# A float32 decoder block on one core: wider runs for the FFN's up tiles, Strassen sums in three batches, and an opening in pieces

## The chip, the cores and the metric

The kernel runs on one core of a Trainium2 chip. Its time is the device time of one execution in microseconds (us), as a median of runs; less is better. The core has a matrix engine (TensorE, PE in the profile, with its weight loads as PEld), a vector engine (VectorE, DVE), an activation engine (ScalarE, ACT), GpSimd (POOL) and SyncE (SP). SP does no arithmetic here: it issues nearly all loads, in order, and each may wait until a buffer is free. Each engine works through its own instructions in order, and they wait for one another by semaphores.

## The reference

One decoder block on 256 tokens of width 2048, all in float32. `c` gives six vectors (shift, scale and gate of both halves) by a product with a 2048 x 12288 matrix; the rest is three large products with pointwise work between them.

```python
mod = jax.nn.silu(c) @ w_ada[l] + b_ada[l]
sh1, sc1, g1, sh2, sc2, g2 = jnp.split(mod, 6, axis=-1)
h = modulate(rms_norm(x, norm1_g[l]), sh1, sc1)
proj = h @ w_in[l]                                  # 2048 x 6144: q, k, v, gb, gc, xt
...                                                 # attention over the one block of 256; short gated convolution
x = x + g1[:, None, :] * (mixed @ w_out[l])         # 2048 x 2048
h2 = modulate(rms_norm(x, norm2_g[l]), sh2, sc2)
u = causal_dwconv(h2 @ w_ffn_up[l], ffn_conv_w[l], ffn_conv_b[l])   # 2048 x 11264, 3 taps
u_gate, u_up = jnp.split(u, 2, axis=-1)
ffn = (jax.nn.silu(u_gate) * u_up) @ w_ffn_down[l]  # 5632 x 2048
x = x + g2[:, None, :] * ffn
```

## The kernel before

**Slots.** All large products run weight tile by weight tile. A tile holds 4 blocks of 128 x 512 (1 MB) in a `raw` buffer; there are seven. ACT rounds it to `hi` (`split_hi`, L329), DVE subtracts to get `lo` (`split_lo`, shown as L166, the line through which most DVE work is issued), and PE multiplies hi by hi, hi by lo and lo by hi. There are three `hi` and three `lo` buffers, and both are made two slots ahead. Such a tile is a slot; the program has 228. PE's order is the order of the slots, written out before anything is issued. All other work is put at a slot by `at(slot, f)`, and within a slot the table `cls` sorts it. The tables in `CFG` thus set the order on every engine.

**Loads.** `want` queues an issue, `load_next` issues one when a buffer comes free, and SP issues in that order. `x_first` and the table `ada` decide how the tiles of `w_ada` (read for the six vectors) are mixed into those of the slots. A `w_ada` tile is multiplied on PE (`ada` L396) or added up on DVE (`ada` L389).

**The opening.** Scale and shift of the first half (SC1, SH1) come first, for two of the 16 row blocks only (256 columns): two tiles of 1 MB each, 8 x 128 x 256 values per partition. PE sums them into 4 x 32 equal rows, ACT copies the sums (`adae`), PE transposes them (`adac`), DVE reduces the transposed rows to two columns (`adaz`), and ACT adds the shift to `hf` to get `h`. The products of slot 0 (`mc`, L583) follow, first with the halves of the first weight tile that are rounded by then.

**The FFN's up products.** `w_ffn_up` has 22 groups of 256 columns on the gate side and 22 on the up side. A unit is one group of both: each of its tiles is loaded by two DMAs of 512 KB (runs of 1 KB), and four such tiles (2048 rows) fill four PSUM banks `z` (L1048, L1063, L1066). PSUM has eight banks. Behind a unit's last product, `up_sum` copies the right half of each bank by ACT and adds the left by DVE (`ub`), which frees the bank. Then both sides are convolved (`up_conv`, `up_conv_b`: `uy`, `tap`), the gate side goes through silu, and `up_gate` multiplies.

**The down products by Strassen.** Groups 0 to 15 go through one level of Strassen's scheme: per group and per half of the output columns (cp 0, 1) an A slot with three products and a B slot with four, which sum over a batch of groups in three or four PSUM banks `u`. At the end of a batch the banks are copied (`pu`, L940) and added to `down_sums` in DRAM by POOL's DMAs. `join_load` reads the sums back on SP, `join_sum` combines them. These slots stand between up slots. The last twelve tiles are ordinary products for groups 16 to 21, and the evacuation of the last bank ends the program.

## Time and profile before

| | |
|---|---|
| median of 3 runs | 1145.72 us (1144.72 to 1145.93) |
| profiled execution | 1145.98 us, of which the span 1144.2 us |
| mean granted PE clock | 0.997 |
| PE, PEld | 1129.7 us (99%), 954.1 us (83%) |
| DVE | 1064.4 us (93%), 1167 instructions |
| ACT | 731.6 us (64%), 1091 instructions |
| POOL | 61.5 us (5%) |
| DMA | 198687 packets, 363.66 MB, mean 318 GB/s |

A busy time is the time in which the engine has an instruction running, and its share is of the span. Matmuls overlap in PE, so "mean ns of one" is longer than the distance from one to the next. A row of a group gives line, engine, operation, output and inputs by name, count, busy us, mean ns of one, and the idle time just before, with what ended it. A window's row gives for each engine its busy time, then PE's granted clock, the busy share of the 16 DMA engines and GB/s.

### The profile page before, as it was taken

To read this page: it belongs to the slowest core of one execution; us is meant where nothing else is said; L and a number is where in the kernel's file an instruction comes from. 1 tells how busy PE (TensorE), PEld (TensorE's weight loads), DVE (VectorE), ACT (ScalarE), POOL (GpSimd) and SP (SyncE) were. 2 spreads that over 40 slices of the span, in tenths; PEclk is the share of its full clock that TensorE was granted. 3 is DMA by queue.
4 is the path that set the end of the run, shared out by engine and by line. 5 is a ranking of instruction groups with operands and counts; after the bars stand their busy time and mean duration, and the time that the engine had idled before them with its cause. 6 is when DMAs were issued, how large, how long until landed. Compare 5 with 4: busy or idle time off the path is not lost.

```text
span 1144.2 us, 16252 instructions
## 1 busy us (share of the span) xinstructions
PE 1129.7 (99%) x6035; PEld 954.1 (83%) x6035; DVE 1064.4 (93%) x1167; ACT 731.6 (64%) x1091; POOL 61.5 (5%) x90
## 2 busy tenths in 40 slices
PE   6999999999999999999999999999999999999998
PEld 4777778888888879988888888888888888888887
DVE  4789989989999998889999999899999999999798
ACT  4644455576786555566687676776677768866731
POOL 1000000000000000000000000101011101111000
PEclk8999999999999999999999999999999999999999
DMA  9999998998998899987679887999899988999951
GB/s 361 407 412 397 412 371 302 408 382 308 331 397 314 290 317 359 325 278 245 213 246 369 305 293 248 310 360 299 313 272 340 317 317 265 351 313 303 367 222 74
DMA packets 198687, 363.66 MB, mean 318 GB/s; under 512 B 9408, under 2 KB 108180, under 8 KB 194000
## 3 DMA queue, kind: packets, MB, share of 16 engines
q1 hardware_dynamic: 189152, 343.44, 82.8%
q0 software_dynamic: 8160, 17.04, 6.9%
q10 hardware_dynamic: 1296, 2.16, 0.6%
q8 instruction: 47, 0.77, 0.2%
q14 instruction: 32, 0.26, 0.1%
HBM read 343.70 MB, written 18.89 MB: 317 GB/s over the span
## 4 chain that ended last, share of the span: by engine, by line
PE 94%; DVE 2%; DMA 2%; issue 1%; ACT 1%; SPq 0%; DVEq 0%; ACTq 0%
PE z L1063 24%; PE z L1066 13%; PE u L1002 4%; PE u L1004 4%; PE u L1000 4%; PE z L1048 4%; PE ada L396 1%; DVE lo L166 1%; PE mx L516 1%; PE mq L516 1%; PE mg L516 1%; PE mk L516 1%; PE mx L517 1%; PE mv L516 1%; PE mg L517 1%; PE mq L517 1%
## 5 line engine op out<-in xcount | busy, mean ns | idle before, releaser
L329 ACT ACTIVATE hi<-raw 128x2048 fp32r<-128x2048 f32 (+1 forms) x227 | 417.6, 1857 | 263.6 <-DMA raw<-in_w_in_dram 73.5
L166 DVE TENSOR_TENSOR lo<-raw,hi 128x2048 fp32r<-128x2048 f32 (+2 forms) x229 | 501.6, 2200 | 23.3 <-ACT hi L329 23.1
L1063 PE MATMUL z<-h,hi 128*128 128x512 f32 x1280 | 303.3, 390 | 0.3 <-DVE ub L166 0.3
L1063 PEld LDWEIGHTS z<-h,hi 128*128 128x128 f32 x1280 | 237.8, 188 | 49.5 <-ACT hi L329 0.8
L389 DVE SCALAR_TENSOR_TENSOR ada<-raw,csil,ada 128x512 f32<-128x512 f32 (+3 forms) x167 | 195.7, 1175 | 5.3 <-DMA raw<-in_w_ada_dram 1.8
L1066 PEld LDWEIGHTS z<-h,lo 128*128 128x128 f32 x1280 | 163.1, 191 | 5.6
L1066 PE MATMUL z<-h,lo 128*128 128x256 f32 x1280 | 165.0, 283 | 0.0
L1002 PE MATMUL u<-hi,gh 128*128 128x512 f32 x224 | 88.1, 394 | 0.1
L1004 PE MATMUL u<-hi,gl 128*128 128x512 f32 x224 | 87.7, 392 | 0.0
L1000 PE MATMUL u<-lo,gh 128*128 128x512 f32 x224 | 61.4, 390 | 0.0
L812 ACT ACTIVATE uy<-ub,fc,fc 128x256 f32<-128x256 f32 x88 | 47.6, 599 | 11.9 <-DVE ub L166 11.9
L944 POOL DMA_DIRECT2D down_sums<-pu x42 | 36.7, 1290 | 304.3 <-ACT pu L940 304.3
L1002 PEld LDWEIGHTS u<-hi,gh 128*128 128x128 f32 x224 | 42.2, 188 | 10.0 <-ACT pu L940 2.9
L1000 PEld LDWEIGHTS u<-lo,gh 128*128 128x128 f32 x224 | 41.9, 188 | 9.2 <-DVE lo L166 0.3
L1004 PEld LDWEIGHTS u<-hi,gl 128*128 128x128 f32 x224 | 42.2, 189 | 7.5
L1048 PE MATMUL z<-h,hi 128*128 128x256 f32 x256 | 46.6, 284 | 0.4 <-ACT h L771 0.2
L823 ACT ACTIVATE tap<-ub,fc 128x256 f32<-128x256 f32 x96 | 41.7, 504 | 0.0
L1048 PEld LDWEIGHTS z<-h,hi 128*128 128x128 f32 x256 | 40.0, 192 | 0.8 <-ACT h L771 0.5
L166 DVE TENSOR_TENSOR ub<-z,ub 128x256 f32<-128x256 f32 x96 | 33.8, 414 | 7.2 <-ACT ub L844 7.1
L301 DVE TENSOR_TENSOR raw<-raw 128x1024 f32<-128x1024 f32 x32 | 38.9, 1217 | 1.2 <-DMA raw<-in_w_ffn_down_dram 1.2
L844 ACT ACTIVATE ub<-z 128x256 f32<-128x256 f32 x96 | 28.6, 383 | 12.7 <-PE z L1063 12.7
L1048 PE MATMUL z<-h,lo 128*128 128x256 f32 x128 | 36.2, 283 | 0.0
(460 smaller groups left out, 1787.3 us busy)
## 6 DMA issues: line engine op xcount, KB each, us to landing
raw<-in_w_ada_dram SPq DMA_DIRECT2D x96, 1024.0 KB, 7.4
raw<-in_w_ffn_up_dram SPq DMA_DIRECT2D x176, 512.0 KB, 6.1
raw<-in_w_in_dram SPq DMA_DIRECT2D x47, 1024.0 KB, 8.1
...
raw<-in_w_ffn_down_dram SPq DMA_DIRECT2D x32, 512.0 KB, 4.9
...
```

The source lines that it names most:

```text
L166: f(*a, **k)
L329: act(hi[:, :n], t[:, :n], AF.Copy)
L389: W.scalar_tensor_tensor(out=self.acc, in0=t[:, j, :], scalar=csil[:, i:i + 1], in1=self.acc, op0=ALU.mult, op1=ALU.add)
L516: mm(o, a, hi[:, k, s], start=(first and k == 0), stop=False)
L812: act(y[:, s], b[:, s], AF.Identity, bias=bias[:, i + j:i + j + 1], scale=w[2][:, i + j:i + j + 1])
L823: act(z[:, s], b[:, s], AF.Copy, scale=w[2 - d][:, i + j:i + j + 1])
L1000: mm(bank_of(key), a, lo[:, n], start=False, stop=j in ends)
L1002: mm(bank_of(key), a, hi[:, n], start=key not in begun, stop=False)
L1004: mm(bank_of(key), b, hi[:, n], start=False, stop=False)
L1048: mm(o, w[:, j, a], h2T[k + j][:, v * 256:v * 256 + 256], start=begins and j == 0 and w is hi and not v, stop=ends and j == 3 and w is lo)
L1063: mm(zp[grp][ft], hi[:, j, ft * P:(ft + 1) * P], h2T[k + j], start=begins and j == 0, stop=ends and j == 3 and not late)
L1066: mm(zp[grp][ft][:, :256], lo[:, j, ft * P:(ft + 1) * P], h2T[k + j][:, :256], start=False, stop=ends and j == 3 and late)
```

## The change

It has three parts and a new set of tables.

- **Up tiles.** A unit is now one side of two neighbouring groups: 512 neighbouring columns, one DMA of 1 MB per tile in runs of 2 KB, 88 of them in place of 176. Even units hold the gate side, odd units the up side of the same two groups. `up_sum`, `up_conv`, `up_silu` and `up_gate` are rewritten for it: a unit is followed by the convolution of both groups and, on the gate side, two silu, on the up side two products. The second tap of the gate side's convolution goes from DVE to ACT from group 6 on (`taps`).
- **Strassen batches.** Three batches of 6, 5 and 5 groups in place of four of 4: 12 half sets end in place of 16, with 42 copies `pu` in place of 56. Which Strassen slots follow which up tile (`places`) is new, and the loads and adds of the join come at other slots.
- **Opening.** The second shift tile is loaded in two pieces, and each is multiplied as it lands (`products`). Its row sums are turned into columns by two PE products with a vector `sel` in place of the two transposes and DVE's reduce, and DVE adds the first shift. The first weight tile is loaded in four pieces of 256 KB, and its four blocks are rounded by ACT and DVE in turns. `hf` is made earlier. Thirteen products of `onesr` with itself into an unused bank (`keep_busy`) stand in PE's order between the opening's products: nine behind the first scale tile, four behind the second.

All other tables (`gate_rows`, `turns`, `up`, `cls`, `x_first`, `hi_late` and so on) have new values. The number and shape of all other PE products is unchanged.

```diff
-                 [[0, 1, 2, 3], [4, 5, 6, 7], [8, 9, 10, 11], [12, 13, 14, 15]], [[0, 'A'], [1, 'A'], [0, 'B'], [1, 'B']],
+                 [[0, 1, 2, 3, 4, 5], [6, 7, 8, 9, 10], [11, 12, 13, 14, 15]], [[0, 'A'], [1, 'A'], [0, 'B'], [1, 'B']],
...
-       'join': [[-5, 1], [-2, 6]],
+       'join': [[-6, 0], [0, 4]],
-       'taps': [1, 1, 2, 6],
+       'taps': [1, 2, 2, 6],
-       'up': [[0, 2, 2, 4], [0, 0, 0, 0]],
+       'up': [[0, 1, 2, 6], [0, 2, 1, 4], [0, 1, 1, 3], [0, 0, 0, 0]],
+       'busy': [9, 4, 0],
+       'norm_at': [1, 6, 6],
...
+        def products(self, r, i, j):
+            if i == 0:
+                self.used += 1
+                self.held = self.view(take((self, r)))
+            if self.acc is None:
+                self.acc = bank(f"ada{self.part}_{self.c0}")[:, :self.n]
+            for k in range(i, j):
+                q = 32 * (k % 4)
+                mm(self.acc[q:q + 32, :], crep[:, self.rows * r + k, :], self.held[:, k, :],
+                   start=r == 0 and k < 4, stop=r == self.tiles - 1 and k >= self.rows - 4,
+                   tile_position=(0, q))
+            if j == self.rows:
+                load_next()
...
+            if not slots_begun:
+                slots_begun.append(f)
+                for j in range(4):
+                    a = (COL[f] + j % 2) * 512
+                    nc.sync.dma_start(t[:, j], w_in[0, (k + j // 2) * P:(k + j // 2 + 1) * P, a:a + 512])
+                return
...
-    def up_sum(grp, one):
+    def up_sum(u, one):
+        g, w = u // 2 * 2, u % 2
+        new = (g, w) not in ub
...
-    def conv_half(grp, w):
+    def up_conv(grp, w):
+        u = grp // 2 * 2 + w
+        y = uy[grp, w] = t2k(f"uy{grp}")
+        conv3(ub.pop((grp, w)), y, fcols[:3], fcols[3], w * 44 + 2 * grp, CFG["taps"][1 + w] if grp >= CFG["taps"][3] else 0)
...
-            slots.append((w_load(w_up, k, 4, [(grp * 256, 256), (DFF + grp * 256, 256)]), 4, go))
+            slots.append((w_load(w_up, k, 4, [(grp % 2 * DFF + grp // 2 * 512, 512)]), 4, go))
...
-            for n, f in zip(lag, (up_conv, up_conv_b, up_silu, up_gate)):
-                at(UP_SLOTS[-1] + 1 + hold + n, f, grp)
+            w = grp % 2
+            for n, (f, *a) in zip(lag, ((up_conv, 0, w), (up_conv, 1, w), (up_gate if w else up_silu, 0), (up_gate if w else up_silu, 1))):
+                at(UP_SLOTS[-1] + 1 + hold + n, f, grp - w + a[0], *a[1:])
...
+    ada_init[1].cuts[1] = [(0, 4), (4, 8)]
+    def keep_busy(b, n):
+        for _ in range(n):
+            mm(b[:, 256:384], onesr, onesr, start=True, stop=True)
...
+    sh.products(1, 0, 4)
+    keep_busy(p_one, w2)
+    sh.products(1, 4, 8)
+    rows_sum = t2k("adae")[:, :256]
+    act(rows_sum, sh.acc, AF.Copy)
+    for k in range(2):
+        mm(p_one[:, k:k + 1], rows_sum[:, k * P:(k + 1) * P], sel, start=k == 0, stop=k == 1)
+    z = small(8, "adaz")[:, :2]
+    V.tensor_copy(z, p_one[:, :2])
...
-    if CFG["first_hi"]:
-        V.tensor_copy(hi[:, s], w[:, s])
-    z, _ = ada_init[1].cols(True)
-        act(hT[k][0], h, AF.Identity, bias=z[:, k:k + 1])
+    act(hi[:, 0], w[:, 0], AF.Copy)
+            V.tensor_scalar(hT[k][0], hf[k], z[:, k:k + 1], None, op0=ALU.add)
+    V.tensor_copy(hi[:, 1], w[:, 1])
+    act(hi[:, 2], w[:, 2], AF.Copy)
+    V.tensor_copy(hi[:, 3], w[:, 3])
```

PE in the opening, from the second shift tile to the first products of slot 0, before:

```order
L396 MATMUL ada_0_219<-raw,crep 32x256 [waits DMAHW7_49]
L396 MATMUL ada_0_219<-raw,crep 32x256 x7
L453 MATMUL adac_0_268<-ident,adae_0_256 128x128 [waits Activation_49]
L453 MATMUL adac_0_268<-ident,adae_0_256 128x128
L583 MATMUL mc_293<-hi,h_261 128x512 [waits Activation_49]
L583 MATMUL mc_294<-hi,h_261 128x512 [waits PE_49]
L583 MATMUL mc_293<-hi,h_261 128x512 [waits DVE_49]
L583 MATMUL mc_294<-hi,h_261 128x512
L583 MATMUL mc_295<-hi,h_261 128x512
```

The same piece of the changed kernel (`one` is the bank of the `sel` products):

```order
L382 MATMUL ada_0_242<-raw,crep 32x256 [waits DMAHW7_49]
L382 MATMUL ada_0_242<-raw,crep 32x256 x3
L382 MATMUL ada_0_242<-raw,crep 32x256 [waits DMAHW0_49]
L382 MATMUL ada_0_242<-raw,crep 32x256 x3
L1577 MATMUL one<-sel,adae 128x1 [waits Activation_49]
L1577 MATMUL one<-sel,adae 128x1
L607 MATMUL mc_313<-hi,h_283 128x512 [waits DVE_49,Activation_49]
L607 MATMUL mc_314<-hi,h_283 128x512
L607 MATMUL mc_313<-hi,h_283 128x512 [waits DVE_49]
L607 MATMUL mc_314<-hi,h_283 128x512
L607 MATMUL mc_315<-hi,h_283 128x512 [waits DVE_49]
```

The eight shift products now wait for two loads, and `sel` products stand where the transposes stood.

SP's queue in the opening, from the tile of slot 3 to the `w_ada` tile that PE multiplies in the middle of `mq`, before (every row is 1 MB; `w_in` for slots, `w_ada` for the six vectors):

```order
L545 DMA raw<-in_w_in_dram 128x2x1024 [waits DMAHW6_49,PE_49]
L363 DMA raw<-in_w_ada_dram 128x8x256 [waits DMAHW7_49,PE_49]
L363 DMA raw<-in_w_ada_dram 128x8x256 [waits DMAHW0_49,DMAHW1_49,DVE_49,Activation_49]
L545 DMA raw<-in_w_in_dram 128x2x1024 [waits DMAHW2_49,DVE_49]
L363 DMA raw<-in_w_ada_dram 128x4x512 [waits DMAHW3_49,DVE_49]
L545 DMA raw<-in_w_in_dram 128x2x1024 [waits DMAHW5_49,PE_49]
L363 DMA raw<-in_w_ada_dram 128x4x512 [waits DMAHW4_49,DVE_49]
L363 DMA raw<-in_w_ada_dram 128x4x512 [waits DMAHW6_49,DVE_49]
L545 DMA raw<-in_w_in_dram 128x2x1024 [waits DMAHW0_49,PE_49]
L545 DMA raw<-in_w_in_dram 128x2x1024 [waits DMAHW7_49,DVE_49]
L363 DMA raw<-in_w_ada_dram 128x4x512 [waits DMAHW1_49,DVE_49]
```

The same places of the queue in the changed kernel (as many MB are ahead of the first row):

```order
L370 DMA raw<-in_w_ada_dram 128x8x256 [waits DMAHW1_49,PE_49]
L569 DMA raw<-in_w_in_dram 128x2x1024 [waits DMAHW2_49,PE_49]
L370 DMA raw<-in_w_ada_dram 128x8x256 [waits DMAHW4_49,DMAHW3_49,DVE_49]
L569 DMA raw<-in_w_in_dram 128x2x1024 [waits DMAHW5_49,DVE_49]
L370 DMA raw<-in_w_ada_dram 128x4x512 [waits DMAHW6_49,DVE_49]
L569 DMA raw<-in_w_in_dram 128x2x1024 [waits DMAHW0_49,PE_49]
L370 DMA raw<-in_w_ada_dram 128x4x512 [waits DMAHW7_49,DVE_49]
L370 DMA raw<-in_w_ada_dram 128x4x512 [waits DMAHW1_49,PE_49]
L569 DMA raw<-in_w_in_dram 128x2x1024 [waits DMAHW2_49,DVE_49]
L569 DMA raw<-in_w_in_dram 128x2x1024 [waits DMAHW3_49,DVE_49]
L370 DMA raw<-in_w_ada_dram 128x4x512 [waits DMAHW4_49,DVE_49]
```

One `w_ada` tile that PE multiplies went ahead of the tile of slot 3; the last three rows stand where they stood.

DVE at the end of an up unit with all eight banks in use (the unit's banks are `z_0_7046` to `z_3_7049`; PE's next unit begins with the bank that the first `ub` frees), before:

```order
L166 TENSOR_TENSOR gl_7147<-gs_6658,gh_7126 128x512 [waits Activation_49]
L166 TENSOR_TENSOR lo<-raw,hi 128x2048 [waits PE_49,Activation_49]
L166 TENSOR_TENSOR lo<-raw,hi 128x2048 [waits DMAHW2_49,DMAHW3_49,PE_49,Activation_49]
L389 SCALAR_TENSOR_TENSOR ada_0_4166<-raw,csil,ada_0_4166 128x2048 [waits DMAHW4_49]
L166 TENSOR_TENSOR ub_7229<-z_0_7046,ub_7229 128x256 [waits Activation_49]
L166 TENSOR_TENSOR ub_7229<-z_1_7047,ub_7229 128x256 [waits Activation_49]
L166 TENSOR_TENSOR ub_7230<-z_2_7048,ub_7230 128x256 [waits Activation_49]
L166 TENSOR_TENSOR ub_7230<-z_3_7049,ub_7230 128x256 [waits Activation_49]
```

DVE at the end of unit 7 in the changed kernel (its banks are `z_0_5407` to `z_3_5410`):

```order
L169 TENSOR_TENSOR lo<-raw,hi 128x1536 [waits DMAHW7_49,DMAHW6_49,PE_49]
L169 TENSOR_TENSOR ub_5630<-z_0_5407,ub_5630 128x256 [waits Activation_49]
L169 TENSOR_TENSOR ub_5630<-z_1_5408,ub_5630 128x256 [waits Activation_49]
L169 TENSOR_TENSOR ub_5631<-z_2_5409,ub_5631 128x256 [waits Activation_49]
L169 TENSOR_TENSOR ub_5631<-z_3_5410,ub_5631 128x256 [waits Activation_49]
L169 TENSOR_TENSOR gl_5642<-uy_4917,gh_5640 128x512 [waits Activation_49]
L169 TENSOR_TENSOR gs_5644<-uy_5087 128x256
```

And PE there in the changed kernel, from unit 7's last products to unit 8's second bank:

```order
L1090 MATMUL z_3_5410<-h_12_4539,lo 128x256 x2
L1090 MATMUL z_3_5410<-h_14_4545,lo 128x256 x2
L1087 MATMUL z_0_5665<-h_0_3718,hi 128x512 [waits Activation_49]
L1087 MATMUL z_0_5665<-h_1_3722,hi 128x512
L1087 MATMUL z_0_5665<-h_2_3729,hi 128x512
L1087 MATMUL z_0_5665<-h_3_3733,hi 128x512
L1087 MATMUL z_1_5666<-h_0_3718,hi 128x512 [waits DVE_49]
```

Unit 8 follows unit 7 with no Strassen slot between them, and its second bank waits for DVE.

More of the change, by code (lines that the diff above doesn't have):

```diff
@@ L226, in tile_block @@
     V.tensor_copy(identb, ident)
+    sel = const.tile([P, 1], F32, name="sel")
+    V.tensor_reduce(out=sel, in_=ident.rearrange("p (j r) -> p j r", j=4)[:, :, 0], axis=AX.X, op=ALU.add)
     rows(vb, [(by_p(norm1_g[0]), 16)], nc.gpsimd)
@@ L356, in __init__ @@
             self.used = 0
+            self.cuts = {}
         def want(self, r):
@@ L1504, in tile_block @@
     ada_init[0].consume(0)
+    def keep_busy(b, n):
+        for _ in range(n):
+            mm(b[:, 256:384], onesr, onesr, start=True, stop=True)
+    p_one = bank("one")
+    w0, w1, w2 = CFG["busy"]
+    keep_busy(p_one, w0)
     pr = bank("n1b")
@@ L1517, in xn_norm @@
                             in1=rT.unsqueeze(1).to_broadcast([P, 2, 256]), op=ALU.mult)
-    xn_norm(0, 1, 2, 3)
-    ada_init[0].consume(1)
-    ada_init[0].evac()
-    ada_init[0].cols()
-    xn_norm(4)
+    sc, sh = ada_init
+    n0, n1, n2 = CFG["norm_at"]
+    xn_norm(*range(n0))
+    sc.consume(1)
+    keep_busy(p_one, w1)
+    sc.evac()
+    sc.cols()
+    hf = []
+    b1 = SH1 * NK
+    for k in range(2):
+        hf.append(t1k("hf"))
+        V.tensor_scalar(hf[k], xnT[0][:, k * 256:(k + 1) * 256], A1[:, k:k + 1], bcol[:, b1 + k:b1 + k + 1],
+                        op0=ALU.mult, op1=ALU.add)
@@ L1554, in tile_block, with rest @@
-    for s, _, _ in parts:
-        V.tensor_tensor(out=lo[:, s], in0=w[:, s], in1=hi[:, s].bitcast(F32), op=ALU.subtract)
+    done.update((SH1, k) for k in range(2))
+    hk = [t2k(f"h{k}", F32R) for k in range(2)]
+    act(hi[:, 0], w[:, 0], AF.Copy)
+    for k in range(2):
+        hT[k] = halves(hk[k])
+        if k:
+            act(hT[k][0], hf[k], AF.Identity, bias=z[:, k:k + 1])
+        else:
+            V.tensor_scalar(hT[k][0], hf[k], z[:, k:k + 1], None, op0=ALU.add)
+    def rest(k):
+        V.scalar_tensor_tensor(out=hT[k][1], in0=hf[k], scalar=z[:, k:k + 1], in1=hT[k][0].bitcast(F32),
+                               op0=ALU.add, op1=ALU.subtract)
@@ L1556, in tile_block @@
+    rest(0)
+    V.tensor_copy(hi[:, 1], w[:, 1])
+    rest(1)
+    act(hi[:, 2], w[:, 2], AF.Copy)
+    V.tensor_copy(hi[:, 3], w[:, 3])
+    xn_norm(*range(n1, n2))
+    for j in range(0, 4, 2):
+        V.tensor_tensor(out=lo[:, j:j + 2], in0=w[:, j:j + 2], in1=hi[:, j:j + 2].bitcast(F32), op=ALU.subtract)
+    xn_norm(*range(n2, 8))
     splits.append((hi, lo))
```

132 lines of the change are left out of this document (57 added, 75 removed), and 16 rows, old and new, of the table CFG.

## The prediction

> **What bounds the kernel now.** I read the page first: busy shares, the chain that ended last, and the two groups of products for which PE idled in the middle of the program.
>
> ```profile
> PE 1129.7 (99%) x6035; PEld 954.1 (83%) x6035; DVE 1064.4 (93%) x1167; ACT 731.6 (64%) x1091; POOL 61.5 (5%) x90
> ...
> PE 94%; DVE 2%; DMA 2%; issue 1%; ACT 1%; SPq 0%; DVEq 0%; ACTq 0%
> ...
> L1063 PE MATMUL z<-h,hi 128*128 128x512 f32 x1280 | 303.3, 390 | 0.3 <-DVE ub L166 0.3
> L1048 PE MATMUL z<-h,hi 128*128 128x256 f32 x256 | 46.6, 284 | 0.4 <-ACT h L771 0.2
> ```
>
> PE carries 94% of the chain and is busy 99% of 1144.2 us. DVE, at 93%, is not far behind. The last two rows say how little PE stood still once the FFN began: 0.3 us behind DVE's `ub` adds, 0.4 us behind `h`. Then the busy times by stage (PE, PEld, DVE, ACT, POOL, granted clock, DMA share, GB/s):
>
> ```profile
> 0.00:25.00 25.00, 14.58 (x110) 9.61 (x111) 9.78 (x28) 11.39 (x17) 5.26 (x16) 0.93 0.96 356
> 25.00:50.00 25.00, 25.00 (x126) 18.98 (x126) 20.73 (x26) 14.41 (x19) 0.00 (x0) 0.94 1.06 402
> ...
> 300.00:600.00 300.00, 299.62 (x1771) 262.15 (x1770) 283.94 (x379) 193.73 (x327) 6.45 (x10) 1.00 0.85 299
> 600.00:900.00 300.00, 299.71 (x1594) 257.90 (x1593) 290.05 (x282) 216.56 (x273) 23.37 (x31) 1.00 0.95 313
> ```
>
> PE lacks 10.42 us in the first 25, and 0.38 and 0.29 us in two stretches of 300. So time can be won from waits in the opening and, at most, 0.67 us from 300 to 900; a larger gain there would need less PE work, and the change keeps the products. Time can be lost everywhere, since any new wait of PE is paid in full. So next I read the chain through the opening, and PE's granted clock (its column behind POOL's) in two pieces of it.
>
> ```profile
> 20.61 1.29 DVE xnT L166 x2
> 21.90 0.64 DVE hf L166 x2
> 22.55 0.60 DVE hi L166
> 23.15 0.09 DVE adaz L166
> ...
> 23.26 0.52 ACT h L1548
> ...
> 23.82 7.41 PE mc L583 x24
> ...
> 24.00:26.00 2.00, 2.00 (x7) 1.45 (x8) 1.14 (x3) 1.11 (x2) 0.00 (x0) 0.67 1.02 420
> 26.00:28.00 2.00, 2.00 (x6) 1.61 (x5) 1.91 (x3) 1.91 (x1) 0.00 (x0) 0.50 1.04 383
> ```
>
> The first slot's products (`mc`) begin at 23.82 behind a string of DVE work, and run 1.66 us longer than at full clock (0.33 and 0.50 of two 2 us pieces).
>
> **Part 1: the opening up to the first product.** These are the last shift products and three operations of the first weight tiles in time order (start, length, engine), ending with a later `ada` product:
>
> ```profile
> 20.73 1.07 PE L396 MATMUL ada<-raw,crep 128*32 128x256 f32 x16
> 21.86 0.38 ACT L417 ACTIVATE adae<-ada 128x256 f32<-128x256 f32 x1 [4.02 <-PE ada L396]
> 22.30 0.44 PE L453 MATMUL adac<-ident,adae 128*128 128x128 f32 x2 [0.50 <-ACT adae L417]
> ...
> 57.02 1.92 ACT L329 ACTIVATE hi<-raw 128x2048 fp32r<-128x2048 f32 x1 [0.84 <-DMA raw<-in_w_in_dram]
> 59.60 1.92 ACT L329 ACTIVATE hi<-raw 128x2048 fp32r<-128x2048 f32 x1 [0.67 <-DMA raw<-in_w_in_dram]
> ...
> 62.61 1.06 PE L396 MATMUL ada<-raw,crep 128*32 128x512 f32 x8
> ```
>
> In the changed kernel half of the shift tile's eight products are done before its second piece lands. No row gives that landing, but the products begin at 20.73 right behind transposes, so it was no later; 0.54 us of products (half of 1.07) then end at 21.27 at the latest. Behind them: the copy to `rows_sum` 0.38, two products with `sel` 0.44 at most (the transposes that they replace), a copy to `z` that I put at 0.1, as the `adaz` reduce took, and `h` on DVE at 0.5 (ACT's `h` took 0.52). With 0.2 for the hand-overs (an estimate, 0.06 stands between 20.73 + 1.07 and 21.86) that is 22.9, against 23.82: 0.9 us sooner. Both `hf` and the rounding of the weights no longer stand between. If the piece lands sooner, up to half a microsecond more: I take 1.1 for the first product, between 0.9 and 1.4. The thirteen `one` products fill PE's gaps there and delay nothing that PE alone would otherwise hold.
>
> That gain does not reach the end. The rows at 57.02 and 59.60 are roundings of two neighbouring 1 MB tiles in SP's queue, each begun the moment its tile landed: one MB in 2.58 us. The `ada` tile behind them is next in the queue (SP's rows in the section on the change: two `w_in` tiles, then `w_ada`), so it landed near 59.60 + 2.58 = 62.18, and PE used it at 62.61. In the changed kernel the same tile stands in the same place, behind the same bytes, and PE has the same products ahead of it. However early PE begins, it stands there until about 62.18. The stream can hardly come sooner:
>
> ```profile
> GB/s 417 424 406 420 413 398 384 385 385 385 423 430 383 388 385 385 385 425 432 401 404 424 424 406 394 410 404 410 429 419 417 410 413 408 410 406 419 424 417 424
> DMA packets 9228, 18.77 MB, mean 408 GB/s; under 512 B 301, under 2 KB 4397, under 8 KB 9225
> q1 hardware_dynamic: 9225, 18.73, 104.4%
> ```
>
> From 20 to 66 us the queue is 104.4% busy at a mean of 408 GB/s. So the opening is worth 0.4 us (0 to 0.6), whatever the first product and the clock do. Where the stall goes is plain: into that wait of PE for the tile, on which DVE and ACT do not depend. The 0.4 us is also the most by which later work can run ahead.
>
> **Part 2: up tiles of one side of two groups.** The products are the same in number and shape. What changes is DVE and ACT work and the runs of the loads. These are the priced groups (count, busy us and mean ns):
>
> ```profile
> L166 DVE SCALAR_TENSOR_TENSOR uy<-ub,fc,uy 128x254 f32<-128x254 f32 x56 | 24.5, 478 | 0.6
> L166 DVE TENSOR_TENSOR uy<-tap,uy 128x510 f32<-128x510 f32 x32 | 21.8, 682 | 0.3 <-ACT tap L823 0.2
> L823 ACT ACTIVATE tap<-ub,fc 128x256 f32<-128x256 f32 x96 | 41.7, 504 | 0.0
> L940 ACT ACTIVATE pu<-u 128x512 f32<-128x512 f32 x56 | 28.8, 592 | 3.1 <-PE u L1000 3.0
> L166 DVE TENSOR_TENSOR uy<-uy,uy 128x512 f32<-128x512 f32 x22 | 15.0, 683 | 0.1
> raw<-in_w_ffn_up_dram SPq DMA_DIRECT2D x176, 512.0 KB, 6.1
> ACT hi L329 <- DMA raw<-in_w_ffn_up_dram: 6.4, 3, 4.2
> ```
>
> The second conv tap of the gate side (`taps` 1 to 2) moves from DVE to ACT: DVE loses 32 of the 478 ns operations (15.3 us) and gains 16 of 682 (10.9), so 4.4 us less; ACT gains 32 of 504 (16.1). ACT at 64% has room, and DVE's 4.4 us are spread over stretches in which PE lacks 0.67 in all: they win a little cover and no time. The up loads become 88 of 1 MB in place of 176 of 512 KB. ACT waited for up loads 6.4 us in three places, and no row of PE's waits names them, so faster loads are worth nothing and slower ones are covered.
>
> **Part 3: Strassen sums in three batches.** The half sets that end go from 16 to 12: 14 fewer copies `pu` of 592 ns (8.3 us of ACT) and 14 fewer DMAs on POOL, which idles. PE does not wait for POOL. The last sums, though, end four slots later, so that the join's loads and adds come nearer the end; the end itself is the last twelve standard tiles, whose evacuation is unchanged. SP's queue stands at the join's loads until the last sums are written, and the weight tiles queued behind them wait too; the raw buffers already hold the tiles of the next slots, and with that cover I cost it at nothing. Without it one tile comes late by about the 2.58 us that a load takes in the stream.
>
> **Part 4: the order around a unit's end.** Here a stall goes and one may come. In the kernel before, PE waited at a place where four `z` and four `u` banks fill PSUM, and the next unit's first bank comes from DVE's adds:
>
> ```profile
> 777.94 4.48 DVE L166 TENSOR_TENSOR lo<-raw,hi 128x2048 fp32r<-128x2048 f32 x2
> 782.34 2.34 DVE L389 SCALAR_TENSOR_TENSOR ada<-raw,csil,ada 128x2048 f32<-128x2048 f32 x1
> 784.61 1.41 DVE L166 TENSOR_TENSOR ub<-z,ub 128x256 f32<-128x256 f32 x4
> 785.08 3.92 PE L1063 MATMUL z<-h,hi 128*128 128x512 f32 x16 [0.29 <-DVE ub L166]
> ...
> L166 DVE TENSOR_TENSOR lo<-raw,hi 128x1536 fp32r<-128x1536 f32 x32 | 55.7, 1751 | 3.8 <-ACT hi L329 3.8
> ```
>
> DVE's `ub` came behind two `lo` and an `ada` step of 2.34 us, and PE stood 0.29 us. Such unit ends stay in the changed kernel, but there are fewer half sets, each that ends has up products behind it, and other work stands ahead of `ub`. I take half of the 0.67 us as gone, 0.3 (0 to 0.7), since some of it belongs to `h` and stays.
>
> New is the end of unit 7: unit 8 follows with no Strassen slot between, while three `u` banks are in use, so that one bank alone is free. PE's second bank there waits for DVE's first add, which stands behind a `lo` of 1.75 us. PE has 0.95 us of products in the free bank before it needs the second (four at 303.3 / 1280 = 0.237), and the four adds last 1.41 us together, less than PE takes for two banks. So it costs nothing if that `lo` is through when unit 7 ends, and 1.75 at most if it has just begun. The nearest row is the same sort of wait at 785.08, 0.29 us: I take 0.3, between 0 and 1.8.
>
> **The sum**: -0.4 (opening) - 0.3 (waits gone) + 0.3 (new wait) = -0.4 us. The profiled execution took 1145.98 us (1144.2 of span and 1.8 around it), which gives 1145.6; it lies 0.26 above the median of the runs, 1145.72, so against the median I predict 1145.3. What a measurement of this kernel can tell from no change is about 0.2%, 2.3 us: faster is below 1143.4, slower above 1148.0.
>
> **Rivals.**
>
> A, faster: the opening's gain reaches the end because the stream lands sooner. For it speaks that the row of GB/s moves between 383 and 432; at 432 throughout, the 18.77 MB from 20 to 66 us take 43.4 us in place of 46, so 2.6 us less. PE could use it: 1.1 from the first product and 1.66 if the clock is no longer halved, 2.8. With the waits gone that is 1145.7 - 2.6 - 0.3 = 1142.8. Against it: the same queue, the same bytes, and pieces of the first tiles that are smaller, not larger.
>
> [...]
>
> B, slower: DVE's work now comes in pairs. Each odd unit closes both groups of its pair, so its two `uy` products (683 ns each) stand together where there was one per unit, ahead of `lo`. At the busiest stretch there is no room left beside DVE:
>
> ```profile
> 525.00:550.00 25.00, 25.00 (x147) 22.17 (x147) 25.00 (x35) 16.83 (x26) 0.00 (x0) 1.00 0.70 230
> ```
>
> Eleven odd units by 0.68 us is 7.5 us if nothing covers it; with half of them covered 3.7, so 1149.4. Against it: DVE has 4.4 us less to do, and buffers for three `lo`. It decides from the point where four units lose a whole 0.68 us (2.3 / 0.68 = 3.4).
>
> C: the change does not do what it says. The first product comes no earlier because the shift tile's second piece lands late, and the waits of the middle only move: 1145.7.
>
> **How the numbers follow.** The forecast has 0.50, A 0.22, B 0.20, C 0.08. The first and the last lie within 0.2%: same 0.58; faster 0.22; slower 0.20. The forecast by itself spans 1144.5 (everything gained that the rows allow) to 1147.0 (the new wait at its upper bound). The range goes into A and B until about 0.1 is left out on each side: 1142.6 to 1149.0.
>
> **What would show it.** In the profile after: the first `mc` product near 22.7; PE's granted clock full or not from 24 to 28; at the `ada` product in the middle of `mq` (62.61 before) an idle wait of PE or of its weight load for the `w_ada` tile, and its start between 62.0 and 62.3; PE busy at least 299.5 of 300 in the middle stretches; no wait for `ub` at the end of unit 7 above 1.8 us. If that `ada` product starts before 61.5, rival A is right. If PE's idle time behind `lo` or `ub` sums to over 2 us, B is.

## The result, and the profile after

The changed kernel took 1162.44 us (median of 5 runs, 1161.78 to 1165.32), the kernel before 1145.93 in the same comparison (1144.72 to 1146.67): a ratio of 1.0149, 95% interval 1.0134 to 1.0164. It is slower by 16.5 us where 0.4 less was forecast, far outside the range given. The profiled execution took 1165.32 us, 1163.5 of it span, so its rows show some 3 us more than the median. One execution of a later run (old grid and early gate) took 5574.18 us at a granted clock of 0.191 and is left out below; with it that run's median is 1151.58, the 1151.6 of the expectations, and without it 1150.60.

From the page, busy shares, chain and the two `z` groups, as they were shown of before:

```profile
PE 1138.9 (98%) x6050; PEld 960.2 (83%) x6050; DVE 1064.3 (91%) x1154; ACT 736.6 (63%) x1109; POOL 49.6 (4%) x76
...
PE 74%; DVE 14%; DMA 8%; issue 2%; ACT 1%; POOL 0%; DVEq 0%; SPq 0%; ACTq 0%; POOLq 0%
...
L1087 PE MATMUL z<-h,hi 128*128 128x512 f32 x1280 | 304.9, 391 | 2.8 <-DVE ub L169 2.7
...
L1072 PE MATMUL z<-h,hi 128*128 128x256 f32 x256 | 46.6, 284 | 0.4 <-ACT h L795 0.2
```

PE's share of the chain fell from 94% to 74%, and DVE and DMA took 14% and 8%. That alone shows little, since a second profile of before has 78, 10 and 6%. DVE has as much busy time as before (1064.3 against 1064.4), and a `z` product takes as long (391 ns, 390 before). PE waits more. The busy times by stage, the same four as of before:

```profile
0.00:25.00 25.00, 17.34 (x121) 11.92 (x121) 7.90 (x26) 10.33 (x16) 5.26 (x16) 1.00 0.97 334
25.00:50.00 25.00, 23.97 (x120) 18.15 (x121) 19.27 (x28) 13.46 (x17) 0.00 (x0) 0.93 1.06 377
...
300.00:600.00 300.00, 298.87 (x1772) 261.52 (x1772) 283.15 (x375) 191.44 (x325) 4.79 (x7) 1.00 0.84 299
600.00:900.00 300.00, 295.01 (x1558) 253.62 (x1557) 279.86 (x265) 214.53 (x281) 16.30 (x24) 0.99 0.84 292
```

The last column of the first two rows is the one to see: 334 and 377 GB/s, against 356 and 402 before, with a DMA share as full as it was (0.97 and 1.06). The queue is as busy and brings 6% less. From 600 to 900 us PE lacks 4.99 us, where it lacked 0.29 (1.76 in the second profile of before). The waits of PE from 300 us to the end (in all, times, longest):

```profile
PE m('D', 0)0_9915 L535 <- DVE lo L169: 3.0, 1, 3.0
PE z L1087 <- DVE ub L169: 2.7, 1, 2.7
PE u L1026 <- DVE ub L169: 1.4, 1, 1.4
PE n2b L768 <- DVE n2d L169: 0.8, 1, 0.8
PE z L1090 <- DVE lo L169: 0.6, 1, 0.6
```

The loss thus shows in four places: the load stream, the end (`m` is the last standard tiles), unit ends (`z`, `u`), and the first norm of the FFN (`n2b`, the products that spread the norm's factors over the partitions). The experiments take them one at a time.

### The profile page after: what moved, and what is told of

Its sections match the earlier page's. It is cut to its first block, busy times and chain, and to the rows that moved or that the text cites. A ratio compares the mean times of both kernels' runs of the same rounds, so it can differ in the third digit from the quotient of the medians.

```text
span 1163.5 us, 16030 instructions
## 1 busy us (share of the span) xinstructions
PE 1138.9 (98%) x6050; PEld 960.2 (83%) x6050; DVE 1064.3 (91%) x1154; ACT 736.6 (63%) x1109; POOL 49.6 (4%) x76
## 4 chain that ended last, share of the span: by engine, by line
PE 74%; DVE 14%; DMA 8%; issue 2%; ACT 1%; POOL 0%; DVEq 0%; SPq 0%; ACTq 0%; POOLq 0%
PE z L1087 23%; PE z L1090 12%; DVE lo L169 5%; PE z L1072 4%; PE u L1024 4%; PE u L1028 4%; PE u L1026 4%; DMA raw<-in_w_ada_dram 3%; DVE ada L410 3%; DMA raw<-in_w_ffn_down_dram 2%; PE mx L537 1%; PE mv L537 1%; PE mx L538 1%; PE mv L538 1%; PE mx L535 1%
## 5 line engine op out<-in xcount | busy, mean ns | idle before, releaser
L334 ACT ACTIVATE hi<-raw 128x2048 fp32r<-128x2048 f32 (+1 forms) x227 | 418.5, 1856 | 279.9 <-DMA raw<-in_w_in_dram 66.1
L169 DVE TENSOR_TENSOR lo<-raw,hi 128x2048 fp32r<-128x2048 f32 (+2 forms) x229 | 501.3, 2201 | 23.3 <-ACT hi L334 23.2
L847 ACT ACTIVATE tap<-ub,fc 128x256 f32<-128x256 f32 x128 | 54.5, 505 | 0.0
L169 DVE TENSOR_TENSOR uy<-tap,uy 128x510 f32<-128x510 f32 x64 | 43.9, 686 | 3.5 <-ACT tap L847 0.2
L968 POOL DMA_DIRECT2D down_sums<-pu x28 | 24.5, 1290 | 285.5 <-ACT pu L964 285.5
```

The lines of the kernel that those rows point to most:

```text
L169: f(*a, **k)
L334: act(hi[:, :n], t[:, :n], AF.Copy)
L847: act(z[:, s], b[:, s], AF.Copy, scale=w[2 - d][:, i + j:i + j + 1])
```

## The experiments

All ratios are against the kernel before, timed beside it on the same chip. Where no interval is given, the time is a single one.

**Both kernels again.** No edit.

> The kernel before, unchanged, profiled beside the others on this chip. In the first profile of before the 22nd MB of the load stream landed by about 62.2 us; in that of the changed kernel PE met it at 65.8 us, with the queue as busy (share 1.04) and 396 in place of 412 GB/s from 50 to 75 us. Theory 'form' (the smaller pieces and the order of the first tiles slow the stream): here again near 402 to 412 GB/s from 25 to 75 us, the ada product in the middle of mq at 62 to 63 us, time 1145 to 1146.5. Theory 'chip' (the stream's rate differs by chip or execution): near 380 to 396 GB/s and that product at 65 to 66 us, and then the kernel before itself takes 1147 to 1150 here.

> The changed kernel, unchanged, as the base for the edits and for its waits. Theory 'waits' (the loss is a handful of waits that the new order makes): again 1161 to 1165, with PE's waits in the same four places: about 3 us by 150 us, 3 to 4 us behind ub near 660, 2 to 3 us near 860, 4 to 5 us behind lo near 1122, and an end of 5 us behind the last product in place of 3.5. Theory 'chip': the opening's 3 us and the waits near 660 and 860 change by some us from execution to execution, since they hang on when loads land.

Measured: before 1148.05 us (a single time; the median of seven others is 1146.44); after 1162.65 us, ratio 1.0142 (1.0127 to 1.0157). The loss is there again. A second profile of each shows how much of the opening changes by itself. In before, the first slot product came at 22.32 us (23.82 in the first profile); in after at 23.43 (25.34). PE's clock (the third column from the end) of before in its second profile:

```profile
0.00:25.00 25.00, 14.56 (x116) 9.78 (x116) 10.34 (x29) 11.62 (x17) 5.26 (x16) 1.00 0.97 359
25.00:50.00 25.00, 24.18 (x128) 17.80 (x127) 20.80 (x26) 14.71 (x18) 0.00 (x0) 1.00 1.06 402
```

The same program that showed 0.93 and 0.94 now shows 1.00 throughout. The half clock after the opening, on which 1.66 us of rival A rested, comes and goes from run to run. The GB/s do not: 359 and 402 here, 336 and 377 in the second profile of after.

**Without the keep-busy products.**

```diff
-       'busy': [9, 4, 0],
+       'busy': [0, 0, 0],
```

> The changed kernel without its thirteen keep-busy products. Theory 'on the path' (nine of them took 2.1 us and four 0.7 us ahead of the scale's last products and transposes, so hf, the transposes behind it and the last shift products all came late): the first mc product 1.5 to 2.5 us sooner, at 23 to 24 us; the time unchanged within 1 us, since PE meets the 22nd MB of loads anyway. Theory 'clock' (they keep PE at full clock and so win more than they cost): first product as late, half clock longer in mc, time 1 to 3 us longer.

Measured: 1163.49 us, ratio 1.0145 (1.0129 to 1.0162), as with them. The products are not the loss. In the first profile of after they do stand in the chain through the opening:

```profile
11.75 1.93 PE ada L417 x16
13.69 2.11 PE one L1534 x9
15.80 0.96 PE n1b L1543 x4
16.76 1.87 PE ada L417 x16
18.62 0.72 PE one L1534 x4
19.35 0.26 PE adac L474 x2
```

so 2.83 us of them stand ahead of `adac` (19.35 here, 17.89 before). But that profile's first products were slow (the first 16 of `ada` took 1.93 us, in the second profile 1.07, and the thirteen 1.22 and 0.66). With them, the first slot product came at 23.43 in the second profile; without them it came at 23.29. What they delay by themselves is thus small. Nor do they hold the clock. After, with them, was halved:

```profile
26.00:28.00 2.00, 2.00 (x6) 1.61 (x6) 2.00 (x5) 0.46 (x1) 0.00 (x0) 0.50 1.00 396
```

and this run without them was not:

```profile
26.00:28.00 2.00, 2.00 (x11) 1.65 (x10) 2.00 (x4) 0.74 (x1) 0.00 (x0) 1.00 1.00 394
```

In other profiles it is the other way round: 1.00 there in the second profile of after, with them, and 0.96 from 0 to 25 us and 0.97 from 25 to 50 in a run further down without them (old grid, early gate).

**The last gate's sums one slot sooner.** The second pair of `slag` says at which of the last twelve slots, counted from the first, POOL writes the last gate's row sums (`sum_rows`) and reads them back (`spread`): 0 and 3 in the changed kernel, -1 and 2 in before.

```diff
-       'slag': [[2, 2], [0, 3]],
+       'slag': [[2, 2], [-1, 2]],
```

> The changed kernel with the row sums of the last gate (and their spreading) one slot sooner, as in the kernel before, so that POOL sends gate_sums ahead of the last four down_sums. Theory 'waits': the 8 us of DVE for ada<-gate_sums go for the most part, the wait of PE behind lo near 1122 (4.8 us) with them, and the end is 3.5 us again: 4 to 7 us less than the changed kernel. Rival 'DVE is full there': DVE has the same adds to do whichever is first, ends as late, and the time falls by under 2 us.

Measured: 1158.06 us, ratio 1.0103 (1.0088 to 1.0119), 4.6 us less than the second run of after. What happens at the end of after on POOL:

```profile
1090.58 3.50 POOL L968 DMA_DIRECT2D down_sums<-pu  x4 [41.16 <-ACT pu L964]
1092.75 3.29 POOL L454 DMA_DIRECT2D gate_sums<-adar  x4
1104.73 0.56 POOL L460 DMA_DIRECT2D ada<-gate_sums  x1 [8.69 <-DMA gate_sums<-adar]
```

on DVE:

```profile
1114.29 0.69 DVE L169 TENSOR_TENSOR ju<-ju,ada 128x512 f32<-128x512 f32 x1 [8.00 <-DMA ada<-gate_sums]
```

and on PE:

```profile
1124.97 1.65 PE L535 MATMUL m('D', 0)0_9915<-lo,gh 128*128 128x512 f32 x3 [3.01 <-DVE lo L169]
```

POOL issues the gate's writes right behind four adds to `down_sums`; they land late, the read back goes out at 1104.73, and DVE stands 8.00 us for it with a `lo` in its queue behind the join. PE then stands for that `lo`. With the sums one slot sooner, on POOL:

```profile
1085.51 1.98 POOL L454 DMA_DIRECT2D gate_sums<-adar  x4 [36.94 <-ACT adar L452]
1091.17 3.53 POOL L968 DMA_DIRECT2D down_sums<-pu  x4 [3.68 <-ACT pu L964]
1093.39 1.88 POOL L460 DMA_DIRECT2D ada<-gate_sums  x1
```

The writes go ahead of the adds, the read back 11 us sooner, and both waits are gone; a new wait of PE behind `ub` stands in their place, 0.8 us ending at 1083, at `adab` (the products that add up the gate's rows over the partitions).

**The addresses of the load buffers.** As the programs lay their tiles out, the first `raw` buffer starts at byte 30208 of each partition in before and at 30240 in after: the new vector `sel` (one float per partition, 32 bytes with its padding) stands in front of it, and all seven buffers move. Two kernels change nothing else: after with `sel` in the pool of small vectors (first buffer at 32256, like 30208 a multiple of 512), and before with an unused 32-byte tile, cleared once, in `sel`'s place (30240).

```diff
-    sel = const.tile([P, 1], F32, name="sel")
+    sel = small(1, "sel")
```

> The changed kernel with its new one-column vector sel taken from the pool of small tiles. As a constant of its own it had moved everything laid out behind it by 32 bytes: the first raw buffer begins at byte 30208 of a partition in the kernel before, at 30240 in the changed kernel, and at 32256 here (30208 and 32256 are multiples of 512, 30240 is not). In all four profiles of the changed kernel and its edits the load stream ran at 335, 377, 396, 394 GB/s in the first four stretches of 25 us, in both of the kernel before at 357, 402, 412, 410. Theory 'address' (loads into buffers off that grid are slower): 355 to 360, 400 to 403, 410 to 413 GB/s here, the ada product in the middle of mq at 62 to 63 us in place of 65.8, PE's loss by 150 us 2 to 3 us smaller, the waits behind ub near 660 and 860 gone or under 1 us each, and 1151 to 1156 us in all. Rival 'form' (pieces and order of the loads): rates as in the changed kernel, 1161 to 1164.

```diff
+    V.memset(const.tile([P, 1], F32, name="sel"), 0.0)
```

> The kernel before with one unused constant of one column, which moves all that is laid out behind it by 32 bytes and does nothing else but one memset of 128x1. Theory 'address': the stream falls to about 336, 377, 396, 394 GB/s in the first four stretches of 25 us, the ada product in the middle of mq comes at 65 to 66 us, and the kernel takes 3 to 9 us more than before (3 in the opening, the rest where a w_down tile lands late). Rival 'form': rates and time of the kernel before, within 1 us.

Measured: after with the old grid 1157.32 us, ratio 1.0091 (1.0076 to 1.0106), 5.3 us less than after. Before, shifted, 1154.47 us, ratio 1.0060 (1.0044 to 1.0075): it loses 0.6%, some 7 us, by 32 bytes alone. The first three stretches of after with the old grid, and then of before shifted:

```profile
0.00:25.00 25.00, 17.28 (x134) 12.47 (x135) 11.00 (x32) 11.20 (x17) 5.24 (x16) 1.00 0.97 356
25.00:50.00 25.00, 23.03 (x123) 16.94 (x122) 19.32 (x27) 14.66 (x18) 0.00 (x0) 1.00 1.06 402
50.00:75.00 25.00, 24.36 (x113) 17.67 (x111) 21.34 (x23) 15.43 (x21) 0.09 (x1) 1.00 1.04 413
```

```profile
0.00:25.00 25.00, 13.75 (x112) 9.42 (x113) 9.95 (x29) 10.30 (x16) 5.24 (x16) 1.00 0.97 337
25.00:50.00 25.00, 22.13 (x116) 15.74 (x115) 17.93 (x23) 13.74 (x17) 0.00 (x0) 1.00 1.06 377
50.00:75.00 25.00, 24.41 (x115) 18.02 (x114) 20.09 (x22) 16.72 (x24) 0.00 (x0) 1.00 1.04 396
```

The rate goes with the address, in either kernel. The loads alone are slower: the engines took as long on the shifted tiles (`hi` 1856 ns, before 1857; `lo` 2201, before 2200). In the stretch from 10 to 20 us most packets are runs of 1 KB; before, and then after:

```profile
DMA packets 3736, 3.90 MB, mean 390 GB/s; under 512 B 235, under 2 KB 3628, under 8 KB 3736
```

```profile
DMA packets 3627, 3.46 MB, mean 346 GB/s; under 512 B 242, under 2 KB 3619, under 8 KB 3627
```

Before has 108 longer packets there as well. From 10 to 18 us, where neither kernel has any, the rates are 383 and 345 GB/s: the shift costs 10%. From 50 to 75 us, with longer runs, it costs 4% (413 to 396). The traces hold every packet: from 10 to 75 us the median one of 1, 2 and 4 KB takes 46, 84 and 159 ns in before and in after with the old grid, 51, 87 and 164 in after. So a run of each of these lengths took 3 to 5 ns more in after. From 300 to 900 us, where the DMA share is 0.83 to 0.95 and not over 1, the medians of 2 and 4 KB are 84 and 159 in all three.

That says where the time goes. PE's first `z` product came at 426.3 us in before, 432.0 in after, 427.5 in after with the old grid, and 431.5 in before shifted: over 4 us of the 5.3, and over 5 of the 7, are lost ahead of the FFN. To find the grid, `sel` was made the first column of a wider tile, in after:

```diff
-    sel = const.tile([P, 1], F32, name="sel")
+    sel = const.tile([P, 16], F32, name="sel")[:, :1]     # 30272, a multiple of 64
+    sel = const.tile([P, 32], F32, name="sel")[:, :1]     # 30336, of 128
+    sel = const.tile([P, 64], F32, name="sel")[:, :1]     # 30464, of 256, not of 512
```

> The changed kernel with sel made 64 bytes wide, so that the raw buffers begin at byte 30272, a multiple of 64 but not of 128. Theory 'the grid is 64 bytes': stream rates of e5 (356, 402, 413, 405 GB/s in the first four stretches of 25 us) and about 1157. Theory 'the grid is 128 bytes or more': those of the changed kernel (335, 377, 396, 394) and 1161 to 1165.

> The changed kernel with `sel` as the first column of a wider tile, so that the first load buffer starts at byte 30336, a multiple of 128 and not of 256 (30208 before, 30240 in the changed kernel, 30272 in the run with 64 bytes). If the grid that matters is 128 bytes: stream 356, 402, 413 GB/s in the first three stretches of 25 us, time near 1157. If it is 256 or 512: 336, 377, 396 GB/s, time near 1162.

> The same with the first load buffer at byte 30464, a multiple of 256 and not of 512. If the grid is 256 bytes or less: stream 356, 402, 413 GB/s, time near 1157. If it is 512: 336, 377, 396 GB/s, time near 1162.

Measured, a single time each: 1162.78, 1162.51 and 1154.97 us. The second stretch of the run at 128, and of the run at 256:

```profile
25.00:50.00 25.00, 22.52 (x114) 16.61 (x113) 18.16 (x24) 13.12 (x16) 0.00 (x0) 0.93 1.06 376
```

```profile
25.00:50.00 25.00, 24.06 (x128) 18.25 (x127) 19.31 (x27) 14.70 (x18) 0.00 (x0) 0.98 1.06 402
```

In the run at 64 that stretch has 377 GB/s. So the starts at multiples of 256 bytes (30208, 30464, 32256) brought 402 GB/s from 25 to 50 us, the others (30240, 30272, 30336) 377, 377 and 376: among the starts tried, the grid is 256 bytes. The time of a run of 1 KB rose by 51 / 46 = 1.11 off it; by what means was not shown. Only the address written to has moved here.

**Old grid and early gate together**, the base of what follows, and the same without the keep-busy products.

```diff
-       'slag': [[2, 2], [0, 3]],
+       'slag': [[2, 2], [-1, 2]],
-    sel = const.tile([P, 1], F32, name="sel")
+    sel = small(1, "sel")
```

> sel in the small pool, and the row sums of the last gate one slot sooner, which by itself took 4.6 us off the changed kernel. Theories 'address' and 'waits' together: the two gains add, 4 to 5 us less than e5, 1146 to 1151. If both act on the same wait at the end they don't add, and e7 lies within 2 us of e5.

> As e7, without the thirteen keep-busy products. With the slow stream they made no difference (1163.5 against 1162.7), since PE met the 22nd MB of loads anyway. Theory 'stream decides the opening': the same here within 1 us of e7, and PE still waits for that tile until 62 us. Rival 'now the chain decides': with the faster stream the 2 us that they put ahead of the scale count, and e8 is 1 to 2 us faster than e7.

Measured: 1150.60 us, ratio 1.0035 (1.0021 to 1.0048), and 1151.79, 1.0041 (1.0026 to 1.0056): the keep-busy products make no difference here either. The two causes add up within the intervals: of the 1.42% in the second run of after, the one took 0.51% away, the other 0.39%, and both 1.07%. Some 4 us are left. PE's largest waits of the first of the two, from 300 us on:

```profile
PE z L1087 <- DVE ub L169: 1.6, 1, 1.6
PE u L1026 <- DVE ub L169: 1.1, 1, 1.1
PE adab L449 <- DVE ub L169: 0.8, 1, 0.8
PE n2b L768 <- DVE n2d L169: 0.8, 1, 0.8
PE z L1090 <- DVE lo L169: 0.6, 1, 0.6
```

**What is left: tables.** The wait for `ub` near 660 us in after, on DVE:

```profile
658.31 1.23 DVE L306 TENSOR_TENSOR raw<-raw 128x1024 f32<-128x1024 f32 x1 [2.51 <-DMA raw<-in_w_ffn_down_dram]
...
660.91 2.28 DVE L169 TENSOR_TENSOR lo<-raw,hi 128x2048 fp32r<-128x2048 f32 x1
663.37 1.42 DVE L169 TENSOR_TENSOR ub<-z,ub 128x256 f32<-128x256 f32 x4 [0.18 <-ACT ub L869]
```

and on PE:

```profile
663.85 1.55 PE L1087 MATMUL z<-h,hi 128*128 128x512 f32 x3 [2.67 <-DVE ub L169]
```

DVE stands 2.51 us for a `w_ffn_down` tile that it must add up for a Strassen slot; `lo` and `ub` queue behind it, and PE behind `ub`. The place follows a unit with ten Strassen slots (`[0, 0, 0, 1, 2, 2, 2, 2, 2, 3]`); such a slot has fewer products per MB than an up tile, and the load buffers run empty: a tile's lead over its use fell from 11 us at 622 to 0.1 at 647. Two tables were tried on the base: `gate_rows` of before (the slots behind which DVE adds up the `w_ada` tiles of the last gate), and places without the ten; then both in one kernel.

```diff
-       'gate_rows': [3, 10, 18, 22, 30, 32, 33, 45, 49, 53, 54, 57, 59, 68, 72, 75],
+       'gate_rows': [10, 14, 17, 18, 30, 35, 40, 43, 46, 51, 54, 57, 58, 64, 68, 74],
```

> e7 (sel in the small pool, last gate's row sums one slot sooner; 1151.6) with the 16 row tiles of the last gate put at the up tiles where the kernel before has them (gate_rows). In e7 an ada step of 2.35 us stands on DVE right ahead of the ub adds for which PE waits 1.2 to 1.7 us near 850, three row tiles are loaded between and around the ten Strassen slots of unit 8, and POOL's memset for that gate (1.8 us) runs beside DVE's last n2d, which takes 1.29 us in place of 0.29 while PE waits. Theory 'rows': PE's waits near 425, 657, 850 and 861 (0.9, 1.7, 1.2, 0.7 us) go for the most part: 2.5 to 5 us less than e7, 1146.5 to 1149. Rival 'bursts': only the 0.9 us near 425 go, the others stay since the Strassen slots come as thick as before: 1150 to 1151.

```diff
-                 [[], [0, 1], [0, 0, 0, 1, 2, 2, 2, 2, 2, 3], [0, 1, 3], [1, 1, 3], [1, 2, 3], [0, 1, 2, 3],
+                 [[], [0, 1], [0, 0, 1, 2, 2, 3], [0, 1, 1, 2, 3, 3], [1, 1, 2, 3], [1, 2, 3], [0, 1, 2, 3],
```

> e7 with four of the ten Strassen slots of unit 8 moved to units 9 and 10 (places; at most two in a row in units 8 and 9). Theory 'bursts' (w_down tiles of a thick run of short slots land too late, DVE's weight sums wait, ub behind them comes late): the wait near 657 (1.7 us) and DVE's 2.2 us for that w_down tile go, those near 850 stay: 1 to 2.5 us less than e7. Rival 'rows': no change there or a new wait in units 9 and 10: within 1 us of e7.

> Both edits of e9 and e10. If the two theories act at different places the gains add: 1145.5 to 1148. If each alone takes the lateness away, no faster than the better of the two.

Measured: with `gate_rows` 1159.33 us, ratio 1.0122 (1.0105 to 1.0139), some 9 us worse than the base where 2.5 to 5 less were expected; the wait for `n2d` is gone there, and those of `z` behind `ub` and `lo` have grown to 4.3 and 2.1 us. With places 1152.15, 1.0054 (1.0039 to 1.0069): the wait near 657 is gone, and waits of 0.7 and 1.7 us end at 718 and 750 instead. With both 1157.41, 1.0100 (1.0085 to 1.0115). The waits move. It seems that the new tables were made for one another; neither of the two can be put back by itself with a gain.

**The first norm of the FFN.** PE's wait for `n2d` in after goes back to POOL:

```profile
428.49 1.80 POOL L392 MEMSET ada<- 128x2048 f32 x1 [89.23 <-DVE n2r L169]
```

and DVE:

```profile
429.08 1.28 DVE L169 TENSOR_SCALAR n2d<-ident,n2r 128x128 f32<-128x128 f32 x1
```

POOL clears the 128 x 2048 sums of the last gate ahead of their first step (the first entry of `gate_rows`), and `n2d`, 0.29 us elsewhere, ends at 430.36, 0.07 behind the memset. The entry was moved by five slots, on the base:

```diff
-       'gate_rows': [3, 10, 18, 22, 30, 32, 33, 45, 49, 53, 54, 57, 59, 68, 72, 75],
+       'gate_rows': [8, 10, 18, 22, 30, 32, 33, 45, 49, 53, 54, 57, 59, 68, 72, 75],
```

> The changed kernel with `sel` in the small pool and the last gate's sums one slot sooner (the run before of these two gave 1151.6), and the first entry of gate_rows 8 in place of 3, so that POOL's memset of the last gate's 128 x 2048 rows runs five slots later, away from the first norm of the FFN. Theory: the memset beside DVE's n2d made it take 1.29 us in place of 0.29 and PE wait 0.92 us for n2b; so n2d at 0.29 us, no PE wait for n2b, 0.9 us less: 1150.7. Rival: n2d was slow for another reason, or the time is given back behind the next load: n2d at 1.29 still, or 1151.6.

Measured: 1152.91 us, ratio 1.0048 (1.0030 to 1.0067). The cause of this wait is shown, since both `n2d` are short again and the wait is gone:

```profile
L169 DVE TENSOR_SCALAR n2d<-ident,n2r x2: 285/286/288, 423.0 to 424.4; 128x128 f32<-128x128 f32 x2
```

The time is not less, though: the wait for `ub` near 657 is 2.3 us in this profile, 1.6 in that of the base, and one of 1.8 behind it was 1.1. What PE won was given back there. By what means the memset holds `n2d` up was not shown.

**Runs of the up loads, and the old batches.** On the base, up tiles again in two DMAs with runs of 1 KB; and the four batches of before with their places and join slots, under the new units.

```diff
-            slots.append((w_load(w_up, k, 4, [(grp % 2 * DFF + grp // 2 * 512, 512)]), 4, go))
+            slots.append((w_load(w_up, k, 4, [(grp % 2 * DFF + grp // 2 * 512 + e, 256) for e in (0, 256)]), 4, go))
```

> The changed kernel with `sel` in the small pool and the last gate's sums one slot sooner (1151.6, and 1152 in a second run like it), and each up tile again loaded by two DMAs of 512 KB in runs of 1 KB, as before the change; units, products and order stay those of the changed kernel. Theory 1 (the length of the runs is worth nothing, since nothing waits for up tiles): 1151 to 1153, the same waits of PE for `ub` near 656, 851 and 861. Theory 2 (runs of 2 KB are what keeps the buffers full; shorter ones come later): 1154 or more, more waits of ACT for up tiles. Theory 3 (two DMAs on two queues land sooner than one): under 1150.

```diff
-                 [[0, 1, 2, 3, 4, 5], [6, 7, 8, 9, 10], [11, 12, 13, 14, 15]], [[0, 'A'], [1, 'A'], [0, 'B'], [1, 'B']],
+                 [[0, 1, 2, 3], [4, 5, 6, 7], [8, 9, 10, 11], [12, 13, 14, 15]], [[0, 'A'], [1, 'A'], [0, 'B'], [1, 'B']],
...
-       'join': [[-6, 0], [0, 4]],
+       'join': [[-5, 1], [-2, 6]],
```

> The changed kernel with `sel` in the small pool and the last gate's sums one slot sooner, and with the Strassen sums again in four batches of four groups, with the table of places and the join's slots of the kernel before; the up tiles, their units and the opening stay those of the changed kernel. Theory 1 (the waits of PE for `ub` from 640 to 930 us come from the new batches and places, whose short Strassen slots drain the load buffers): these waits go, PE loses under 1 us between 640 and 930, time 1146 to 1148. Theory 2 (they come from the units of one side, whose DVE work comes in pairs of groups, the prediction's rival B): the waits stay in number and size, time 1150 or more.

Measured: with runs of 1 KB 1153.31 us, ratio 1.0054 (1.0034 to 1.0074): no difference from the base that the intervals can tell. By the ratios the longer runs are worth some 2 us, and the intervals reach from nothing to 5. With the old batches 1164.28 us, ratio 1.0150 (1.0126 to 1.0173): some 13 us worse. PE's waits from 600 us on:

```profile
PE u L1024 <- DVE lo L169: 2.4, 5, 1.3
PE z L1087 <- DVE ub L169: 1.7, 2, 0.9
PE u L1026 <- ACT pu L964: 1.0, 2, 0.7
```

and from 300 to 600 PE lacks 3.3 us, 1.1 in the base. The waits do not come from the new batches by themselves. Whether they come from the units of one side is not settled: the old places were made for units of both sides, and no tables were made for the new units with four batches.

**The opening alone.** Before with the new opening (pieces, `sel` in the pool of small vectors, no keep-busy products), all else as it was. Of the diff:

```diff
+    sel = small(1, "sel")
+    ada_init[1].cuts[1] = [(0, 4), (4, 8)]
...
+       'busy': [0, 0, 0],
+       'norm_at': [1, 6, 6],
```

> The kernel before with the changed kernel's opening alone (second shift tile and first weight tile in pieces, sums by `sel`, no keep-busy products), `sel` kept in the small pool so that the first load buffer starts at a multiple of 512 bytes; FFN, Strassen batches and all tables of before. Theory 1 (the opening itself gains 0.7 to 1.4 us, and the loss of the changed kernel lies in the addresses, the gate and the order of the FFN): 0.5 to 1.5 us less than before, 1144.4 to 1145.4 against 1145.9; stream 356, 402, 413 GB/s in the first three stretches of 25 us; first slot product near 22.2 in place of 23.8. Theory 2 (the gain of the opening is swallowed by the wait for the ada tile in the middle of mq, as the prediction's Part 1 had it): 0.4 us less or nothing. Theory 3 (the opening loses by itself): 1148 or more.

Measured: 1147.24 us against 1146.93, ratio 1.0001 (0.9991 to 1.0012): no change. The first product and the `ada` product in the middle of `mq`:

```profile
22.04 2.29 PE L606 MATMUL mc<-hi,h 128*128 128x512 f32 x9 [0.73 <-ACT h L1587]
...
61.88 1.06 PE L416 MATMUL ada<-raw,crep 128*32 128x512 f32 x8
```

They come 1.78 and 0.73 us sooner than in the first profile of before; against the second, where the two came at 22.32 and 61.86, 0.28 and nothing are left. At the end nothing can be measured. No version beats the kernel before.

## Why the prediction was wrong

**Part 1, opening.** The step that failed is "the same tile stands in the same place, behind the same bytes", with "the same queue, the same bytes" as the ground against any other rate. Place and bytes were right, and PE's weight load was released by that tile:

```profile
65.84 0.16 PEld L417 LDWEIGHTS ada<-raw,crep 128*32 128x32 f32 x8 [0.35 <-DMA raw<-in_w_ada_dram]
```

but at 65.84 us, not between 62.0 and 62.3, since the buffers had left the 256-byte grid and the loads took longer (377 GB/s from 25 to 50 us, 402 before). I took the queue's rate from before as a property of the queue. The cause could have been looked for: the diff adds a tile to the constants. The price of the step is 5.3 us in this kernel, some 7 in the kernel before.

On the old grid the first product came at 21.9 to 22.1, sooner than the 22.7 forecast, and what it won did not reach the end (1.0001 for the opening alone), as forecast. But the place was another: the `ada` product came at 62.6 to 63.0 and did not wait for its tile. PE had stood before, 0.3 to 1.4 us for an earlier `w_ada` tile near 36 us. "Delay nothing", of the keep-busy products, held as far as the runs can tell: with and without them the times are the same on either grid.

**Part 2, up tiles.** "Faster loads are worth nothing" was not contradicted: runs of 1 KB cost nothing that the intervals can tell (1.0054 against 1.0035). The taps moved as counted (48 of DVE's products with `fc` in place of 80, 64 adds of `tap` in place of 48), for 2.8 us of DVE where I had 4.4, and other work took that back: 1064.3 us in all against 1064.4.

**Part 3, batches.** The step that failed is "PE does not wait for POOL", with a later end of the sums costed at nothing. POOL's queue holds the writes of the last sums and of the last gate; the gate's came behind four `down_sums`, DVE waited 8.00 us for it, and PE for DVE. My bound from above was one late tile, 2.58 us; the edit of `slag` won back 4.6. That table's move is part of the change, and I did not follow it.

**Part 4, unit ends.** That "a stall goes" did not come true, and the new wait did not come where I put it, at unit 7. It came at the ends of later units (2.67 us near 660, then 1.4 and 0.6), the first of them because a load of `w_ffn_down` was late ahead of `lo` and `ub`; the other two were not followed. 0.3 was forecast, 1.8 the bound; PE's waits there sum to 4.7 in after, 3.3 on the base.

**Rivals.** Rival B has the sign, and its test (over 2 us behind `lo` or `ub`) was met. Its mechanism, pairs of `uy` ahead of `lo`, was not seen: in the wait that was followed, a sum behind a late load, a `lo` and the `ub` stand ahead of PE. Rival A needed a faster stream; it was slower. The clock, its second leg, changes from run to run in one and the same kernel (from 26 to 28 us 0.50 and 1.00 in the two profiles of after). Rival C had the first product no sooner, which was so in after (25.34 and 23.43), but on the old grid it came at 21.9 to 22.1; and C had no loss. Of the 16.5 us, the grid (5.3 alone) and the gate (4.6 alone) were shown to come back in the time, some 12 us when both were put back; the remaining 4 or 5 stand as PE's waits at unit ends (3.3 on the base), at `adab` and at `n2b` (0.8 each). No edit won them back, and their cause as a whole stays open.
